# Moving low-part subtractions and a few sums from GpSimd to VectorE in a hybrid decoder layer

## The chip, the core and the metric

The program runs on one core of one Trainium2 chip. Its metric is the device time of one execution in microseconds (us); the time of the kernel is the median over several executions. A core has five engines with a queue of instructions each: TensorE (PE in the profile; its weight loads, which overlap the products, stand as PEld), VectorE (DVE), ScalarE (ACT), GpSimd (POOL) and SyncE (SP, which here only issues transfers). An engine works its queue in order; an instruction that waits holds up all that stand behind it.

## The reference

One layer for 1024 new prompt tokens and 8 x 4 decode tokens, width 1024:

```python
h = rmsnorm(x, rms1_g) * (1 + sc1) + sh1          # sc, sh, g: adaLN, silu(c) @ w_ada + b_ada
z = h @ w_in + b_in                               # q, k, v, f, GLU a and b, gate_a, gate_b
o = attend(q, k, v, log_sigmoid(z_f))             # 8 heads of 64, forgetting attention
y_a = o @ w_pa
u = glu_a * sigmoid(glu_b)
y_b = silu(layernorm(depthwise_causal_conv(u, 31 taps))) @ w_pb + b_pb
m = sigmoid(gate_a) * y_a + sigmoid(gate_b) * y_b
x = x + g1 * (m @ w_o)
h2 = rmsnorm(x, rms2_g) * (1 + sc2) + sh2
x = x + g2 * ((silu(h2 @ w_gate) * (h2 @ w_up)) @ w_ffn_out)
y = rmsnorm(x, final_g)                           # k, v, log f and the last rows of u go out too
```

The decode tokens attend to 1024 cached rows each, fetched by a page table.

## The kernel before

All data stand transposed: 128 features on the partitions, tokens along the free dimension (1056 columns, in blocks of 384, 384 and 288). To reach fp32 accuracy at a fast rate, each matrix product is made of three fp32r products: a weight tile w is split into a high part wh (rounded by ScalarE, line 315) and a low part wl = w - wh (line 318), the activations likewise into ah and al, and mm3 (lines 327 to 329) adds wh*ah, wh*al and wl*ah. So each weight tile passes through a transfer into wr (three buffers), a cast on ScalarE, a subtraction on VectorE or GpSimd, and then TensorE, whose third product is the first that needs wl. wh and wl have two buffers each, so a tile's low part may be written as soon as TensorE is done with the tile before the last.

The engine of the subtraction is the argument `eng` of split_w, which w_in_tile, gate, glu and branch hand down. A second argument names the queue that issues the transfer of the raw weights (GpSimd's or SyncE's).

The stages in program order: norm and modulation of x; q and k; v and the forget gates; glu(0); the decode attention in two groups (decode_group); glu(1) to glu(3) with gate(15) to gate(10) between; the prompt attention (scores and weighted, 32 units) with conv_ln, the layer norm of the convolution, at three of its units; gate(9) to gate(0) without 7, and four adaLN products among them; branch(1), the convolution's projection with its gate (out_b); gate(7); branch(0), the attention's projection with its gate and the sum of the two branches (out_a); the product with w_o; the FFN. glu also runs the depthwise convolution on VectorE: 30 multiply-adds over 1024 columns per channel tile (line 528, tile acc), marked as of low urgency, to run where VectorE has nothing else. conv_ln needs all four channel tiles.

The instructions don't stand in program order in the queues. The framework plans them: it simulates the program with estimated durations, and gives each engine's instructions in the order of that simulation; split_ahead marks the splits as urgent, so they stand ahead of what the program has before them. Which order results for another assignment of engines can't be read from the code.

out_a works per tile of 128 features and 264 columns on zg, the sigmoid of the gate, which lies in one of four buffers (tag gev): product times zg on VectorE (line 967), plus X(j), the other branch, on GpSimd for the first seven of eight tiles (line 968), high part on ScalarE (969), low part on VectorE (970).

Of the kernel before, what the change touches and what calls it, by code (L numbers as in the profile page):

```python
# [13 lines left out]
OP = mybir.AluOpType  # L14
# [15 lines left out]
KD = D // P  # L30
# [56 lines left out]
def hybrid_step(ctx, tc, xT, cT, vec, bvf, con, stT, ptab, ptabr, kcT, vc, lfc, w_ada, w_in, w_vfa, w_vfb,  # L87
# [132 lines left out]
            pe.matmul(prs[-1][:, to:to + m], ones[:m, :], dg[:m, d:d + m], start=True, stop=True)  # L220
        return prs if n > 512 else prs[0]

    def sumsq(tiles, n, eng=dve):
        s = sm.tile([P, 400], F32, name="ssum", tag="ssum", bufs=2)
        for i, t in enumerate(tiles):
            if i == 0:
                act.activation(s[:, :n], t, AF.Square)
            else:
                q = ev(sm, "sq", 2, (P, 400))
                act.activation(q[:, :n], t, AF.Square)  # L230
                eng.tensor_tensor(s[:, :n], s[:, :n], q[:, :n], OP.add)
        return s


# [260 lines left out]
    def glu(ct):  # L495
        u = cvp.tile([P, UW], F32, name="u", tag="u", bufs=2)
        us = u[:, KL + NP:].rearrange("p (b i) -> p b i", b=DB)
        pool.memset(u[:, 0:KL], 0.0)
        sp.dma_start(us[:, :, 0:KL], stT[ct].rearrange("p (b i) -> p b i", b=DB))
        wb = w_in_tile(12 + ct, pool, pool)  # L500
        sg = []
        for c in range(3):
            n = CH[c][1]
            ps = gemm_a(wb, c)
            t = ev(cvp, "sg", 4)
            act.activation(t[:, :n], ps[:, :n], AF.Sigmoid, bias=V[:, V_BB + ct:V_BB + ct + 1])
            sg.append(t)
        wa = w_in_tile(8 + ct, pool, pool)
        for c in range(3):
            o, n = CH[c]  # L510
            npr = min(n, NP - o)
            ps = gemm_a(wa, c)
            ba = V[:, V_BA + ct:V_BA + ct + 1]
            dve.scalar_tensor_tensor(u[:, KL + o:KL + o + npr], ps[:, :npr], ba, sg[c][:, :npr],
                                     op0=OP.add, op1=OP.mult)
            if n > npr:
                dve.scalar_tensor_tensor(us[:, :, KL:], ps[:, npr:n].rearrange("p (b t) -> p b t", t=DT), ba,
                                         sg[c][:, npr:n].rearrange("p (b t) -> p b t", t=DT),
                                         op0=OP.add, op1=OP.mult)
        act.dma_start(ucp[ct], u[:, NP:NP + KL])  # L520
        act.dma_start(ucs[ct].rearrange("p (b i) -> p b i", b=DB), us[:, :, DT:])
        with tc.high_priority(offset=-3000):
            a = cvp.tile([P, T], F32, name="acc", tag="acc", bufs=2)
            b = V[:, V_DWB + ct:V_DWB + ct + 1]
            wv = V[:, V_DW + ct * KC:V_DW + (ct + 1) * KC]
            dve.tensor_scalar(a[:, :NP], u[:, 0:NP], wv[:, 0:1], b, OP.mult, OP.add)
            for j in range(1, KC):
                dve.scalar_tensor_tensor(a[:, :NP], u[:, j:j + NP], wv[:, j:j + 1], a[:, :NP],  # L528
                                         op0=OP.mult, op1=OP.add)

            pr = cvp.tile([P, DB, KC], F32, name="cpr", tag="cpr", bufs=2)
            as_ = a[:, NP:].rearrange("p (b t) -> p b t", t=DT)
            for t in range(DT):
                dve.tensor_tensor(pr, us[:, :, t:t + KC], wv.unsqueeze(1).broadcast_to([P, DB, KC]), OP.mult)
                dve.tensor_reduce(as_[:, :, t], pr, mybir.AxisListType.X, OP.add)
            dve.tensor_scalar(a[:, NP:], a[:, NP:], b, None, OP.add)
        act.dma_start(acD[ct], a)
# [213 lines left out]
        decode_group(g)  # L751

    glu(1)
    gate(15, pool, pool)
    glu(2)
    gate(14, pool, pool)
    gate(13, pool, pool)
    glu(3)
    for i in (12, 11, 10):
        gate(i, pool, pool)  # L760

    cvp.release()
    dcp.release()
# [3 lines left out]
    def conv_ln(c):  # L767
# [4 lines left out]
            sp.dma_start(t, acD[ct][:, o:o + n])  # L772
            xc.append(t)
        s = sm.tile([P, 400], F32, name="lnsum", tag="ssum", bufs=2)
        pool.tensor_tensor(s[:, :n], xc[0], xc[1], OP.add)
        for ct in (2, 3):
            pool.tensor_tensor(s[:, :n], s[:, :n], xc[ct], OP.add)
        dve.tensor_scalar(s[:, :n], s[:, :n], 1.0 / CW, None, OP.mult)
        pm = ps_st()
        pe.matmul(pm[:, :n], ones, s[:, :n], start=True, stop=True)  # L780
        for ct in range(4):
            dve.tensor_tensor(xc[ct], xc[ct], pm[:, :n], OP.subtract)
        pr = rstd(sumsq(xc, n, pool), n, CW)
        for ct in range(4):
            g = V[:, V_LNG + ct:V_LNG + ct + 1]
            b = V[:, V_LNB + ct:V_LNB + ct + 1]
# [126 lines left out]
    for x in ready:  # L913
        weighted(*x)
    for i in (9, 8, 6, 5, 4, 3, 2, 1, 0):
        gate(i, pool, sp)
        if 3 <= i < 7:
            ada(8 - i, wp, "wr", 3, ps_mm)
    gains(1, V_RMS2, 32)
# [29 lines left out]
    def branch(which, src, w_p, width, out):  # L949
        xs = split_act(src)  # L950
        for j in range(KD):
            w = split_ahead(w_p[j], 4, pool)
            for o in range(0, T, width):
                zg = ev(wp, "gev", 4)[:, :width]
                sp.dma_start(zg, gD[which][j][:, o:o + width])
# [9 lines left out]
    def out_a(j, o, ps, zg):  # L965
        h, l = [merged(o // SUP, r, j)[:, o % SUP:o % SUP + HS] for r in range(2)]
        dve.tensor_tensor(zg, ps, zg, OP.mult)
        (pool if j < KD - 1 else dve).tensor_tensor(zg, zg, X(j)[:, o:o + HS], OP.add)
        act.copy(h, zg)
        dve.tensor_tensor(l, zg, h.bitcast(F32), OP.subtract)  # L970

    branch(1, cvD, w_pb, CW3, out_b)

    gate(7, pool, sp)
    ap.release()

    bp = mkpool(name="bp", bufs=1, side="right")
# [431 lines left out]
```

## Time and profile before

| | |
|---|---|
| time, median of 3 runs | 1636.25 us (1630.43 to 1641.71) |
| the profiled execution: its time, its span | 1629.88 us, 1628.1 us |
| TensorE busy with products | 1564.1 us, 96% of the span |
| VectorE, ScalarE, GpSimd busy | 1048.5, 697.3, 178.2 us |
| granted TensorE clock, mean | 0.992 of full speed |

The span runs from the first to the last instruction; the 1.8 us around it belong to the start and the end of the execution. Busy TensorE time counts products that overlap in its pipeline, so 96% isn't a share of peak. For each wait the profile names what ended it. The chain of work that ended last is followed back from the last instruction, at each step to what released it. Times in views are counted from the span's start.

### The profile page before, as it was taken

Reading aid. Unit: us, or ns where it says so; the run is one execution under the profiler, and the core shown is the slowest. Engines: PE = TensorE matmul, PEld = TensorE weight load, DVE = VectorE, ACT = ScalarE, POOL = GpSimd, SP = SyncE. Lnnn points to the kernel's source line nnn. Section 1 sums busy time; section 2 is a strip of 40 time slices with the busy share of each in tenths; the row PEclk is TensorE's granted clock in tenths of the full one; section 3 lists DMA queues with packets and bytes.
Section 4 is the critical chain, followed back from the end, with each engine's and each line's share of the span. In section 5 each row is a group of like instructions: output and inputs, shape, how many; then the busy total and the mean of one; then the engine's idle time right before and its main releaser. Section 6 shows DMA issues by size and latency. Waiting matters only on the chain.

```text
span 1628.1 us, 29682 instructions
## 1 busy us (share of the span) xinstructions
PE 1564.1 (96%) x11280; PEld 1475.9 (91%) x11280; DVE 1048.5 (64%) x2161; ACT 697.3 (43%) x1398; POOL 178.2 (11%) x147
## 2 busy tenths in 40 slices
PE   6999999999999989999999999999999999999997
PEld 4899978788977878999899989999999999999997
DVE  6942469999888867244559995555555596324644
ACT  4552112121376766434426663333333375224342
POOL 2121022342220101024200000000000000000000
PEclk9999999999999999999999999999999999999998
DMA  9195476777787774453554322222222257424552
GB/s 358 65 305 177 144 218 184 249 243 201 213 235 242 210 211 153 143 175 114 185 175 150 120 88 92 80 79 80 79 79 80 79 184 242 129 82 142 187 178 81
DMA packets 141424, 261.86 MB, mean 161 GB/s; under 512 B 24634, under 2 KB 81594, under 8 KB 140642
## 3 DMA queue, kind: packets, MB, share of 16 engines
q1 hardware_dynamic: 102802, 209.37, 41.0%
q10 hardware_dynamic: 36384, 43.01, 7.6%
q0 software_dynamic: 2096, 7.60, 1.5%
q8 instruction: 88, 1.44, 0.4%
q14 instruction: 54, 0.44, 0.1%
HBM read 206.44 MB, written 53.48 MB: 160 GB/s over the span
## 4 chain that ended last, share of the span: by engine, by line
PE 72%; DVE 12%; DMA 7%; ACT 3%; issue 3%; POOL 2%; SPq 1%; ACTq 0%; DVEq 0%; POOLq 0%
PE mm L1177 25%; PE mm L1278 16%; PE mm L329 7%; PE mm L328 7%; PE mm L327 7%; DVE acc L528 4%; DMA wa<-w_ada 2%; DMA gev<-gD 2%; POOL wl L318 1%; PE ptr L874 1%; PE mm L561 1%; PE mm L560 1%; PE mm L562 1%; DMA sq<-hD 1%; PE ppv L887 1%
## 5 line engine op out<-in xcount | busy, mean ns | idle before, releaser
L327 PE MATMUL mm<-ah,wh 128*128 128x384 f32 (+2 forms) x768 | 252.9, 330 | 8.8 <-ACT gev L384 4.0
L1278 PE MATMUL mm<-f,wo 128*128 128x352 f32 x1584 | 256.8, 323 | 0.0
L1278 PEld LDWEIGHTS mm<-f,wo 128*128 128x128 f32 x1584 | 254.8, 188 | 0.0
L329 PE MATMUL mm<-ah,wl 128*128 128x384 f32 (+2 forms) x768 | 251.5, 329 | 2.2 <-POOL wl L318 2.2
L328 PE MATMUL mm<-al,wh 128*128 128x384 f32 (+2 forms) x768 | 252.6, 329 | 0.0
L1177 PE MATMUL mm<-c,wc 128*128 128x264 f32 x1776 | 235.3, 285 | 1.5 <-ACT gev L1182 0.9
L1177 PE MATMUL mm<-b,wc 128*128 128x264 f32 x1680 | 228.1, 286 | 3.7 <-DVE wc L1135 1.5
L1177 PEld LDWEIGHTS mm<-c,wc 128*128 128x128 f32 x1776 | 224.1, 188 | 2.4 <-ACT gev L1182 1.3
L1177 PEld LDWEIGHTS mm<-b,wc 128*128 128x128 f32 x1680 | 214.7, 189 | 5.1 <-ACT wc L1134 2.0
L528 DVE SCALAR_TENSOR_TENSOR acc<-u,vec,acc 128x1024 f32<-128x1024 f32 x120 | 173.9, 1471 | 1.2
L327 PEld LDWEIGHTS mm<-ah,wh 128*128 128x128 f32 x768 | 145.9, 190 | 18.3 <-issue 5.9
L328 PEld LDWEIGHTS mm<-al,wh 128*128 128x128 f32 x768 | 146.3, 190 | 11.2 <-issue 10.4
L318 POOL TENSOR_TENSOR wl<-wr,wh 128x1024 fp32r<-128x1024 f32 (+1 forms) x44 | 111.8, 2545 | 396.0 <-ACT wh L315 340.9
L1229 DVE TENSOR_TENSOR wo<-wr,wo 128x512 fp32r<-128x512 f32 x108 | 69.7, 646 | 129.5 <-ACT wo L1228 128.9
L329 PEld LDWEIGHTS mm<-ah,wl 128*128 128x128 f32 x768 | 146.1, 190 | 6.3 <-POOL wl L318 3.1
L1134 ACT CAST wc<-wr 128x512 fp32r<-128x512 f32 x144 | 88.6, 621 | 141.4 <-PE mm L1177 132.4
L1228 ACT CAST wo<-wr 128x512 fp32r<-128x512 f32 x108 | 63.2, 585 | 150.6 <-PE mm L1278 143.3
L1135 DVE TENSOR_TENSOR wc<-wr,wc 128x512 fp32r<-128x512 f32 x144 | 98.5, 689 | 36.0 <-ACT wc L1134 35.0
L315 ACT CAST wh<-wr 128x1024 fp32r<-128x1024 f32 (+1 forms) x64 | 59.7, 939 | 93.1 <-PE mm L328 56.6
L192 POOL MEMSET rv<- 128x5 f32 x7 | 0.7, 103 | 746.2 <-DVE rt L210 746.2
L329 PE MATMUL mm<-b,wl 128*128 128x264 f32 x256 | 72.3, 286 | 2.2 <-DVE wl L318 2.2
L327 PE MATMUL mm<-b,wh 128*128 128x264 f32 x256 | 72.9, 285 | 1.3 <-ACT wh L315 1.3
(294 smaller groups left out, 2735.5 us busy)
## 6 DMA issues: line engine op xcount, KB each, us to landing
wr<-w_fi SPq DMA_DIRECT2D x52, 512.0 KB
wa<-w_ada SPq DMA_DIRECT2D x48, 512.0 KB
wr<-w_fo SPq DMA_DIRECT2D x36, 512.0 KB
kt<-kcT SPq DMA_DIRECT2D x64, 256.0 KB
vt<-vc SPq DMA_DIRECT2D x64, 256.0 KB
hD<-h ACTq DMA_DIRECT2D x44, 264.0 KB
wr<-w_in SPq DMA_DIRECT2D x18, 512.0 KB
wr<-w_o SPq DMA_DIRECT2D x16, 512.0 KB
```

Source lines behind the costliest of these rows:

```text
L315: d = act.copy(wh[:, r, :], raw[:, r, :])
L318: eng.tensor_tensor(wl[:, r, :], raw[:, r, :], wh[:, r, :].bitcast(F32), OP.subtract)
L327: pe.matmul(ps[:, :n], wh[:, k, :], xh, start=(k == 0), stop=False)
L328: pe.matmul(ps[:, :n], wh[:, k, :], xl, start=False, stop=False)
L329: pe.matmul(ps[:, :n], wl[:, k, :], xh, start=False, stop=(k == nk - 1))
L528: dve.scalar_tensor_tensor(a[:, :NP], u[:, j:j + NP], wv[:, j:j + 1], a[:, :NP], op0=OP.mult, op1=OP.add)
L1134: act.copy(w[:, 0, :n], raw)
L1135: dve.tensor_tensor(w[:, 1, :n], raw, w[:, 0, :n].bitcast(F32), OP.subtract)
L1177: pe.matmul(ps[:, :HS], w[i][:, r, k * P:(k + 1) * P], x[s][:, k, :], start=(new and k == 0 and j == 0), stop=(k == 3 and j == 2), skip_gr ...
L1228: act.copy(x[:, 0, :], raw)
L1229: dve.tensor_tensor(x[:, 1, :], raw, x[:, 0, :].bitcast(F32), OP.subtract)
L1278: pe.matmul(ps[e][:, :n], w[r][:, k * P:(k + 1) * P], f[x], start=(k0 + k + i == 0), stop=(k0 + k == HT - 1 and i == 2))
```

## The change

Five places hand `dve` where `pool` stood. The transfers that GpSimd's queue issues stay on GpSimd's queue; the first four tiles of q and k (first_w), the second halves of split_shifted and the copies of q and k stay on GpSimd too.

```diff
-    def sumsq(tiles, n, eng=dve):
+    def sumsq(tiles, n):
...
-                eng.tensor_tensor(s[:, :n], s[:, :n], q[:, :n], OP.add)
+                dve.tensor_tensor(s[:, :n], s[:, :n], q[:, :n], OP.add)
...
-        wb = w_in_tile(12 + ct, pool, pool)
+        wb = w_in_tile(12 + ct, dve, pool)
...
-        wa = w_in_tile(8 + ct, pool, pool)
+        wa = w_in_tile(8 + ct, dve, pool)
...
-    gate(15, pool, pool)
+    gate(15, dve, pool)
...
-    gate(14, pool, pool)
-    gate(13, pool, pool)
+    gate(14, dve, pool)
+    gate(13, dve, pool)
...
-        gate(i, pool, pool)
+        gate(i, dve, pool)
...
-        pool.tensor_tensor(s[:, :n], xc[0], xc[1], OP.add)
+        dve.tensor_tensor(s[:, :n], xc[0], xc[1], OP.add)
         for ct in (2, 3):
-            pool.tensor_tensor(s[:, :n], s[:, :n], xc[ct], OP.add)
+            dve.tensor_tensor(s[:, :n], s[:, :n], xc[ct], OP.add)
...
-        pr = rstd(sumsq(xc, n, pool), n, CW)
+        pr = rstd(sumsq(xc, n), n, CW)
...
-        gate(i, pool, sp)
+        gate(i, dve, sp)
...
-            w = split_ahead(w_p[j], 4, pool)
+            w = split_ahead(w_p[j], 4)
...
-        (pool if j < KD - 1 else dve).tensor_tensor(zg, zg, X(j)[:, o:o + HS], OP.add)
+        dve.tensor_tensor(zg, zg, X(j)[:, o:o + HS], OP.add)
...
-    gate(7, pool, sp)
+    gate(7, dve, sp)
```

## Rows read from the trace of the kernel before

**Rows 1.** Busy time by stage; columns: stretch, length, busy us of each engine (instructions)
```profile
244.00:428.00 184.00, 178.97 (x1157) 151.94 (x1154) 181.56 (x193) 36.51 (x58) 55.09 (x22) 0.99 0.75 228
428.00:465.00 37.00, 35.40 (x243) 32.59 (x243) 28.82 (x95) 22.00 (x43) 6.22 (x6) 1.00 0.52 152
465.00:660.00 195.00, 184.16 (x1345) 155.90 (x1339) 147.16 (x472) 131.06 (x270) 25.55 (x21) 0.98 0.70 208
660.00:742.00 82.00, 79.85 (x504) 78.31 (x503) 27.34 (x38) 34.01 (x58) 15.01 (x11) 1.00 0.51 164
742.00:800.00 58.00, 54.02 (x431) 52.52 (x430) 32.55 (x67) 29.52 (x73) 30.89 (x35) 1.00 0.45 136
```

**Rows 2.** What TensorE waited for from 206 to 428 us: total, times, longest
```profile
PE pss L692 <- DMA kt<-kcT: 3.1, 2, 1.9
PE mm L329 <- POOL wl L318: 2.2, 1, 2.2
```

**Rows 3.** What TensorE waited for from 428 to 660 us
```profile
PE mm L161 <- DMA wa<-w_ada: 5.6, 5, 2.5
PE ptr L874 <- DVE ptl L877: 2.7, 3, 2.1
PE pst L780 <- DVE lnsum L778: 1.6, 1, 1.6
```

**Rows 4.** What TensorE waited for from 660 to 800 us
```profile
PE mm L329 <- POOL wl L318: 2.8, 4, 1.2
PE mm L329 <- DVE wl L318: 1.7, 2, 0.9
```

**Rows 5.** The page's span, and its group of the convolution's multiply-adds
```profile
span 1628.1 us, 29682 instructions
...
L528 DVE SCALAR_TENSOR_TENSOR acc<-u,vec,acc 128x1024 f32<-128x1024 f32 x120 | 173.9, 1471 | 1.2
```

**Rows 6.** The chain that ended last, its pieces from 424 to 438 us
```profile
424.72 3.31 DVE acc L528
428.05 3.08 DMA acD<-acc
...
437.34 0.91 PE pst L780 x2
```

**Rows 7.** GpSimd in order of time: start, us, line, operation, idle before
```profile
322.14 16.62 POOL L318 TENSOR_TENSOR wl<-wr,wh 128x1024 fp32r<-128x1024 f32 x1 [16.69 <-ACT wh L315]
...
385.77 3.10 POOL L318 TENSOR_TENSOR wl<-wr,wh 128x1024 fp32r<-128x1024 f32 x1 [16.61 <-ACT wh L315]
```

**Rows 8.** VectorE in order of time, the same stretches
```profile
320.93 15.63 DVE L528 SCALAR_TENSOR_TENSOR acc<-u,vec,acc 128x1024 f32<-128x1024 f32 x13
...
386.54 3.41 DVE L528 SCALAR_TENSOR_TENSOR acc<-u,vec,acc 128x1024 f32<-128x1024 f32 x1
...
390.19 1.27 DVE L528 SCALAR_TENSOR_TENSOR acc<-u,vec,acc 128x1024 f32<-128x1024 f32 x1
```

**Rows 9.** Tile acc, its multiply-adds; columns: shortest/median/longest ns, first and last start
```profile
L528 DVE SCALAR_TENSOR_TENSOR acc<-u,vec,acc x120: 1248/1278/3410, 224.0 to 424.7; 128x1024 f32<-128x1024 f32 x120
```

**Rows 10.** Line 318 on VectorE: durations, and VectorE's idle time before it
```profile
L318 DVE TENSOR_TENSOR wl<-wr,wh x20: 1208/1224/1399, 79.2 to 881.5; 128x1024 fp32r<-128x1024 f32 x20
...
  ACT wh L315: 6.6, 10
```

**Rows 11.** Groups of GpSimd by shape: count, busy, mean ns, idle before
```profile
L318 POOL TENSOR_TENSOR wl<-wr,wh 128x1024 fp32r<-128x1024 f32 x28 | 90.3, 3229 | 326.5 <-ACT wh L315 287.9 <-PE pss L818 15.1 <-DMA vt<-vc 13.2
L318 POOL TENSOR_TENSOR wl<-wr,wh 128x512 fp32r<-128x512 f32 x16 | 21.5, 1347 | 69.6 <-ACT wh L315 52.9 <-PE mm L329 16.6
L968 POOL TENSOR_TENSOR gev<-gev,XA 128x264 f32<-128x264 f32 x16 | 12.9, 813 | 10.5 <-DVE gev L967 6.1 <-ACT b L969 2.8 <-ACT wh L315 1.5
L231 POOL TENSOR_TENSOR ssum<-ssum,sq 128x384 f32<-128x384 f32 x6 | 6.3, 1044 | 5.5 <-ACT sq L230 5.2
```

**Rows 12.** Groups of VectorE by shape, for the prices there
```profile
L1135 DVE TENSOR_TENSOR wc<-wr,wc 128x512 fp32r<-128x512 f32 x144 | 98.5, 689 | 36.0 <-ACT wc L1134 35.0
L394 DVE TENSOR_TENSOR qkl<-gev,qkh 128x384 fp32r<-128x384 f32 x8 | 4.4, 555 | 14.4 <-ACT qkh L393 14.3
L968 DVE TENSOR_TENSOR gev<-gev,XB 128x264 f32<-128x264 f32 x4 | 1.6, 426 | 0.0
```

**Rows 13.** Line 825 on VectorE, a one-column instruction of the attention: shortest/median/longest ns
```profile
L825 DVE SCALAR_TENSOR_TENSOR st<-mx,Cq x64: 190/212/2348, 429.6 to 646.7; 128x1 f32<-128x1 f32 x64
```

**Rows 14.** The chain that ended last, shares of its stretch from 680 to 800 us
```profile
by line: DMA gev<-gD 21.3%; issue 16.1%; PE mm L329 11.6%; PE mm L328 11.4%; PE mm L327 10.4%; ACT b L969 3.4%; DMA gD<-gev 3.3%; ACT gev L956 3.1%; DMA yr<-cvD 3.0%; POOL gev L968 2.7%; POOL wl L318 2.5%; DVE gev L967 2.5%; ACT wh L315 2.5
```

## What the change does to the time, predicted before it ran

> **What bounds the kernel now.** I read the busy time by stage first. In the stages that hold the moved work, from 244 to 800 us, TensorE has an instruction running nearly all the time [rows 1]: 178.97 of 184 us, 35.40 of 37, 184.16 of 195, 79.85 of 82, 54.02 of 58. So the change can win at most TensorE's idle time there, 5.0 + 1.6 + 10.8 + 2.2 + 4.0 = 23.6 us, and only the part that GpSimd or VectorE causes. The second thing to see is VectorE, with 181.56 of 184 us busy in the first of these stages: it is the full engine there, beside a full TensorE, while GpSimd is busy for 55.09 us and idle for most.
>
> Then the waits of TensorE say which of its idle time has to do with the change. From 206 to 428 us it waited 2.2 us for a low part from GpSimd and 3.1 us for pages of the cache [rows 2]; from 428 to 660 us 5.6 us for adaLN weights, 2.7 us for low parts of the attention's probabilities, 1.6 us for the layer norm's sum [rows 3]; from 660 to 800 us 2.8 us for low parts from GpSimd and 1.7 us for those of w_o [rows 4]. The transfers aren't touched. What is named with GpSimd or hangs on it is 2.2 + 1.6 + 2.8 = 6.6 us.
>
> Last the two engines beside each other. A multiply-add of the convolution takes 1278 ns in the median, but 1471 on average, and the longest 3410 [rows 5, 9]. The row at 386.54 shows why: 3.41 us, while GpSimd has its subtraction from 385.77 on; the one at 390.19, with GpSimd idle, takes 1.27 us [rows 7, 8]. The other way round, GpSimd's subtraction at 322.14 takes 16.62 us, while VectorE runs 13 multiply-adds one behind the other from 320.93 to 336.56 [rows 7, 8]. So each of the two holds the other up: both read two tiles in SBUF, and they take turns by whole instructions.
>
> **The change part by part.** Moved are 24 full low parts (8 of GLU, 16 of the gates), 16 half ones (branches), 18 sums of the layer norm and 28 of the first branch: 86 instructions. No transfer moves; GpSimd's transfers now wait for VectorE's low part instead of its own, with three buffers ahead, and I cost that at nothing.
>
> Low parts beside the convolution. 15 of the 24 run between 206 and 428 us. On GpSimd a full one takes 3229 ns on average [rows 11], on VectorE 1224 ns in the median [rows 10]. Added to VectorE: 15 x 1.22 = 18.3 us. Given back: what the multiply-adds were held up, 120 x (1471 - 1278) ns = 23.2 us [rows 5, 9]. Net 4.9 us less. Bounds: 18.3 us more, if nothing is given back, and 23.2 us less, if the new instructions were free. I take the net, since the 3.41 us row stands beside GpSimd's and the 1.27 us row doesn't. On the end it is worth little, as TensorE is full in this stage: I take 1 us, from nothing to 4.9. The wait of 2.2 us goes in full: the part that took 16.62 us would take 1.2, in its place in VectorE's queue.
>
> Layer norm. The chain that ended last runs from the last multiply-add at 424.72 over two transfers and the sums to TensorE's mean at 437.34 [rows 6]. Of the first mean's wait 1.6 us stands with the sum. The three additions ahead of it take about 1.0 us each on GpSimd, as line 231 does (1044 ns), and 0.56 on VectorE (a 128x384 subtraction, 555 ns) [rows 11, 12]: 3 x 0.49 = 1.5 us earlier, if VectorE's queue lets them in at once. I take 1.6 us gone, from 0 to 1.6.
>
> In the attention (428 to 660 us) VectorE gets up to 18 x 0.56 + 6 x 1.22 = 17.4 us more. What it gets back is uncertain. Line 825, an instruction on one column, has a median of 212 ns and a longest of 2348 [rows 13], so it too is held up by GpSimd at times; six low parts by 2.1 us each (2348 - 212) would be 12.8 us, the lower bound is nothing. I take half: 11 us more, most of it in the stage from 465 to 660 us, where VectorE goes from 147 to some 156 of 195 us. TensorE waits for VectorE there by the rows, so some of it shows; bounds 0 and 11 us; I take +2, as 2.7 us is all that it waits for the probabilities' low parts now.
>
> Branches (660 to 800 us). A half low part goes from 1347 to 689 ns, and no longer stands in one queue with the sums; a sum goes from 813 to 426 ns [rows 11, 12]. The wait of 2.8 us loses 2.0 (between 0 and 2.8). The sums stand in a ring of four buffers: a gate's tile is loaded, used, and its buffer freed when line 970 is done. The load of gev is the largest part of the chain here, 21.3% [rows 14], so the ring sets the pace beside TensorE. One turn serves four tiles; 28 sums are seven turns, each shorter by 0.39 us: 2.7 us, at most the 4.0 us that TensorE idles from 742 to 800 us, from which the 1.7 us for w_o's low parts come too [rows 1, 4]. I take 2 (0 to 2.7). Is VectorE full then? 32.55 + 28 x 0.43 + 7 x 0.69 = 49 of 58 us: not quite.
>
> Waits in VectorE's order. On GpSimd a low part that stood waiting for its cast held up nothing else: 287.9 us of idle time ahead of 28 of them [rows 11]. On VectorE the multiply-adds and the attention stand behind it, and TensorE waits for those. VectorE's own low parts cost 6.6 us of idle time over 20 [rows 10], 0.33 us each. The 21 between 206 and 660 us make 6.9 us at that; TensorE is full for most of it. I take +1, from 0 to 6.9.
>
> The sum: -2.2 - 1 - 1.6 + 2 - 2.0 - 2 + 1 = -5.8 us. The profiled execution took 1629.88 us, 1.8 more than its span [rows 5]; it becomes 1624. It lies 6.4 us under the median of the runs shown, 1636.25, and about at their fastest; I put the same distance to the median of the new kernel: 1636.25 - 5.8, some 1630 us.
>
> **The rivals.**
>
> Carried through. The relief of VectorE lets the prompt attention start earlier, and the planned order, which now has all of this work on one engine, fits the run better. For it: VectorE has 181.56 of 184 us busy, and the chain runs over its multiply-adds. The most is TensorE's idle time of 23.6 us less the transfers, 5.6 + 3.1: 14.9 us [rows 1 to 3]. Against it: TensorE is full in 428 to 465 us too. About 1621 us.
>
> Nothing comes through. TensorE's waits go, and others of the same 6 us take their place, as the queues are planned anew; for it speaks that TensorE is full everywhere, against it that the waits of [rows 2, 4] have one cause, GpSimd, that is gone: 1635 us.
>
> VectorE is full, and GpSimd's help is gone. The Trainium skill, "Perfetto Trace Analysis", section "Optimizing Scalar/DVE Operations", says that where VectorE is saturated, giving some of its work to GpSimd may make sense, though the two share a read port and it might not help; this change does the reverse. In rows: 18.3 us are added to a stage in which VectorE has 2.4 us free, and if nothing is given back, the layer norm and the attention come 16 us later. TensorE has 35 us of work in 428 to 465 us to run meanwhile, so I count half: +8, less the 6 of the other terms' gains, plus what the attention lacks then, 7: about 1645 us. The row of 3.41 us speaks against it.
>
> Slower: VectorE stands waiting for casts. The place is VectorE's queue from 206 to 660 us, with 21 low parts planned by estimated times. With w us of waiting each, the convolution ends 15w - 4.9 later and the attention loses 6w. Up to w = 0.3 that is hidden; at w = 1.5 it is 17.6 + 9 less 6: 20 us slower, 1656 us. From about 1.3 on it is over 1%. For it: GpSimd idled some 10 us per low part for the casts; against it: the 0.33 us of VectorE's own.
>
> **How the numbers follow.** Forecast 0.48, carried through 0.22, nothing 0.14, VectorE full 0.06, waiting for casts 0.10. One per cent, 16 us, is about what a measurement of this kernel can tell from no change, as its runs lie from 1630.43 to 1641.71 us. Faster by more: 0.20, most of the second case. Slower by more: 0.12, the last case and a little of the fourth. Within 1%: 0.68. The range goes from 1612 us, under the second case by half the spread of the runs shown and a little more, to 1645 us, the fourth; left out are the last case and the tails, some 0.18.
>
> **What the profile would show.** If the steps hold: no multiply-add of line 528 over 1.5 us, its mean within 30 ns of its median; line 318 on VectorE at 1.2 us; GpSimd busy for under 5 us from 244 to 428 us; the last multiply-add some 5 us earlier, against the stages ahead of it; no wait of TensorE for a low part over 1 us between 206 and 800 us; the stage with gev's ring some 2 us shorter. If VectorE waits for casts, its idle time ahead of line 318 is above 20 us in total. The prediction is wrong if multiply-adds stay long with GpSimd idle, if the attention's stage grows by more than 5 us, or if the planned order moves a stage as a whole, which nothing here can show beforehand.

## The result, and the profile after

The changed kernel took 1639.91 us (median of 20 executions, 1633.84 to 1646.41), the kernel before 1630.57 us beside it (20 executions, 1626.06 to 1641.71): a ratio of 1.0051, with a 95% interval of 1.0038 to 1.0063. By this ratio it is slower by 8.3 us (the two medians lie 9.3 us apart). The forecast was 5.8 us faster: the time lies within its range, the sign is wrong.

First the busy time of the changed kernel by stage, in the columns of [rows 1] (the last stage of before lies 8 us earlier):

```profile
244.00:432.00 188.00, 184.46 (x1206) 158.67 (x1207) 169.52 (x204) 38.25 (x61) 3.45 (x8) 1.00 0.75 224
432.00:469.00 37.00, 35.16 (x255) 28.90 (x255) 27.50 (x93) 19.02 (x39) 0.10 (x1) 1.00 0.71 209
469.00:669.00 200.00, 186.34 (x1339) 163.60 (x1337) 148.99 (x485) 128.15 (x263) 0.21 (x2) 0.97 0.67 191
669.00:700.00 31.00, 21.05 (x110) 19.15 (x109) 13.09 (x25) 18.64 (x33) 0.00 (x0) 0.78 0.37 109
700.00:750.00 50.00, 50.00 (x307) 49.67 (x306) 24.29 (x37) 19.91 (x34) 0.00 (x0) 1.00 0.54 167
750.00:808.00 58.00, 58.00 (x478) 58.00 (x477) 45.08 (x109) 32.16 (x77) 0.00 (x0) 1.00 0.52 158
```

Two branches are called the first in the texts on record: branch(0), where the 28 sums are meant, and branch(1), which runs before it, where the input is meant that line 944 splits. Here they go by their numbers.

Two stages stand out. The last, with branch(0)'s sums, has TensorE busy for 58.00 of 58 us, where it was 54.02 [rows 1]: that is the gain that was forecast. The fourth, 31 us around the end of the attention, has it busy for 21.05, at a granted clock of 0.78. The kernel before has nothing like it. Its own attention ends at 672 us (here 687), and of the 31 us around that, in the same columns, TensorE has 30.05, at full clock:

```profile
662.00:693.00 31.00, 30.05 (x192) 28.79 (x191) 9.69 (x13) 14.52 (x23) 2.94 (x3) 1.00 0.54 175
```

What the prediction said of the durations of single instructions came out. The span, the convolution's multiply-adds (page and tile acc, as [rows 5, 9]), line 825 (as [rows 13]) and, for later, the idle time of VectorE ahead of low parts (as [rows 10]), in the changed kernel:

```profile
span 1632.3 us, 29602 instructions
L528 DVE SCALAR_TENSOR_TENSOR acc<-u,vec,acc 128x1024 f32<-128x1024 f32 x120 | 150.0, 1282 | 0.7
L528 DVE SCALAR_TENSOR_TENSOR acc<-u,vec,acc x120: 1247/1282/1294, 218.2 to 431.3; 128x1024 f32<-128x1024 f32 x120
L825 DVE SCALAR_TENSOR_TENSOR st<-mx,Cq x64: 189/210/221, 434.0 to 670.3; 128x1 f32<-128x1 f32 x64
  ACT wh L315: 34.4, 24
```

With GpSimd nearly idle no multiply-add is longer than 1294 ns (it was 3410), and the one-column instruction of line 825 no longer than 221 ns (it was 2348). So GpSimd did hold VectorE up, and now it doesn't. And yet the last multiply-add ended at 432.6 us instead of 428.0.

To see where TensorE's time went I worked out its loss by stretch: for each product the distance to the start of the next, less what the same form of product usually takes in the trace of before (a third of its distances there are shorter), summed. It holds the waits and the half-speed stretches alike. "Around its end" runs from 15 us before the last weighted sum of the attention to 15 us behind the first product of branch(1). Each is one profiled execution:

| us lost by TensorE | up to decode | decode, convolution | attention | around its end | branches | rest | sum |
|---|---|---|---|---|---|---|---|
| before | 34.2 | 47.1 | 49.6 | 3.7 | 6.7 | 26.4 | 167.7 |
| after | 30.5 | 46.7 | 53.6 | 15.6 | 0.9 | 25.7 | 173.0 |

The sums differ by 5.3 us, the ends of the last products by 4.2. Ahead of decode the 3.7 us are no more than the scatter of single executions: e4 below, whose edit leaves that stretch alone, lies as far from the kernel before there. Of the rest, +11.9 us lie around the end of the attention, +4.0 in the attention, -5.8 in the branches. The +4.0 isn't clear of the scatter either: e4, e17 and e18 below have TensorE's order of before up to the branches, and lose 48.6 to 53.7 us in the attention. The profiled execution of the changed kernel, 1634.07 us, is a quick one: it shows about half of the 8.3 us. The other half goes with the mean granted clock, 0.982 over its 20 executions and 0.985 in the profiled one, against 0.988 for the kernel before over all executions beside these studies.

What happens at that end: TensorE of the changed kernel in order of time, all its pieces there that have a wait ahead of them (start, length, line, idle time and what ended it), and its stretch cut finer:

```profile
670.50 0.52 PE L874 MATMUL ptr<-con,px 128*128 128x128 f32 x3 [1.22 <-DVE st L825]
676.76 0.58 PE L886 MATMUL ppv<-pth,vh 128*128 128x256 f32 x1 [3.78 <-ACT pth L876]
679.77 1.11 PE L874 MATMUL ptr<-con,px 128*128 128x128 f32 x4 [0.85 <-DVE ptl L877]
684.49 0.39 PE L887 MATMUL ppv<-ptl,vh 128*128 128x256 f32 x1 [0.19 <-DVE ptl L877]
686.98 0.39 PE L886 MATMUL ppv<-pth,vh 128*128 128x256 f32 x1 [1.13 <-DVE ot L898]
690.41 2.13 PE L327 MATMUL mm<-yh,wh 128*128 128x352 f32 x6 [2.74 <-ACT yh L944]
```

```profile
669.00:676.00 7.00, 2.77 (x22) 2.28 (x20) 2.67 (x9) 6.89 (x14) 0.00 (x0) 0.99 0.32 94
676.00:683.00 7.00, 5.38 (x24) 4.68 (x25) 3.10 (x7) 5.17 (x11) 0.00 (x0) 0.52 0.04 9
683.00:690.00 7.00, 3.32 (x23) 2.59 (x21) 2.94 (x6) 3.00 (x6) 0.00 (x0) 0.96 0.47 140
690.00:697.00 7.00, 6.59 (x24) 6.59 (x25) 3.02 (x3) 2.50 (x3) 0.00 (x0) 0.55 0.54 167
```

The last units' chain (scores, maximum, exponential, transpose, weighted sum) and then the split of branch(1)'s input (line 944) have nothing of TensorE's to run beside them. In the 7 us from 669 TensorE is busy for 2.77, and in the next 7 the granted clock is 0.52, that is mostly the lower level, 1.2 GHz; it happens again from 683 to 697. So each gap is paid twice. The Trainium skill ("TensorE: Matmul & The Clock Gate", section "HAM oscillation — how this bites in real kernels") says of a long wait that the work behind it starts at the lower clock; this trace agrees, with 0.52 and 0.55.

Why nothing is there can be counted in TensorE's order of instructions. The gates' products (2232 ahead of gate 7's, which come later in both kernels) are what fills the attention. In the kernel before, 160 of them stand behind the attention's last score product and 45 behind its last weighted sum. In the changed kernel there are none behind either. The plan places each product at its estimated earliest time, and in the changed kernel they were all used up earlier.

### The profile page after: what moved, and what is told of

It is laid out like the page before. It is cut to its first block, busy times and chain, and to the rows that moved or that the text cites. A ratio compares the mean times of both kernels' runs of the same rounds, so it can differ in the third digit from the quotient of the medians.

```text
span 1632.3 us, 29602 instructions
## 1 busy us (share of the span) xinstructions
PE 1563.7 (96%) x11280; PEld 1478.4 (91%) x11280; DVE 1056.9 (65%) x2247; ACT 699.3 (43%) x1398; POOL 38.3 (2%) x61
## 4 chain that ended last, share of the span: by engine, by line
PE 81%; DMA 6%; DVE 5%; SPq 3%; issue 2%; ACT 2%; POOL 0%; ACTq 0%; DVEq 0%
PE mm L1177 26%; PE mm L1278 16%; PE mm L327 9%; PE mm L329 9%; PE mm L328 9%; DMA wa<-w_ada 3%; PE ptr L874 1%; SPq L631 1%; SPq L632 1%; PE mm L561 1%; PE mm L560 1%; PE mm L562 1%; PE ppv L887 1%; PE pss L815 1%; PE mm L161 1%
## 5 line engine op out<-in xcount | busy, mean ns | idle before, releaser
L528 DVE SCALAR_TENSOR_TENSOR acc<-u,vec,acc 128x1024 f32<-128x1024 f32 x120 | 150.0, 1282 | 0.7
L318 DVE TENSOR_TENSOR wl<-wr,wh 128x1024 fp32r<-128x1024 f32 (+1 forms) x60 | 64.5, 1080 | 34.7 <-ACT wh L315 34.4
L327 PE MATMUL mm<-b,wh 128*128 128x264 f32 x256 | 72.7, 285 | 0.5 <-ACT wh L315 0.5
L328 PE MATMUL mm<-b,wh 128*128 128x264 f32 x256 | 72.4, 283 | 0.0
```

The lines of the kernel that those rows point to most:

```text
L318: eng.tensor_tensor(wl[:, r, :], raw[:, r, :], wh[:, r, :].bitcast(F32), OP.subtract)
L327: pe.matmul(ps[:, :n], wh[:, k, :], xh, start=(k == 0), stop=False)
L328: pe.matmul(ps[:, :n], wh[:, k, :], xl, start=False, stop=False)
```

## The experiments

Each kernel ran in five rounds beside the kernel before; us against it are the ratio times the median of before in those runs. "Left" counts the gates' products in TensorE's order behind the last score product and, of these, behind the last weighted sum. "End" and "attention" are TensorE's losses as above, in the one profiled execution.

| kernel | moved to VectorE | left | us against before (95%) | attention, end: us lost |
|---|---|---|---|---|
| before | nothing | 160, 45 | | 49.6, 3.7 |
| after | all | 0, 0 | +8.3 (6.2 to 10.3) | 53.6, 15.6 |
| e1_glu_gates | GLU, six early gates | 12, 0 | +6.7 (3.9 to 9.5) | 49.7, 11.7 |
| e2_layer_norm | 18 sums of the layer norm | 164, 51 | +7.0 (4.4 to 9.8) | 66.7, 2.8 |
| e3_late_gates | ten late gates | 58, 0 | -0.3 (-2.6 to 2.0) | 48.3, 10.5 |
| e4_branches | branches | 160, 45 | -5.0 (-7.3 to -2.6) | 49.8, 3.1 |
| e5_means | 9 sums of the means | 107, 0 | +7.2 (4.2 to 10.1) | 53.5, 11.7 |
| e6_squares | 9 sums of squares | 192, 58 | -3.1 (-6.5 to 0.2) | 53.6, 2.1 |
| e7_loads_ahead | 18 sums, loads 3 units ahead | 167, 52 | +12.1 (7.7 to 16.5) | 68.0, 2.4 |
| e8_gates_held | all, gates 1 and 0 behind unit 26 | 119, 0 | +8.6 (5.5 to 11.7) | 62.7, 10.9 |
| e9_gates_last | all, gate 1 behind unit 28, 0 behind 31 | 144, 72 | 0.0 (-2.8 to 2.8) | 64.4, 1.6 |
| e10_means_gates_last | e5 held as e9 | 144, 72 | +2.6 (0.5 to 4.9) | 58.6, 3.3 |
| e11_all_but_means | all but the means | 19, 0 | -2.3 (-4.6 to 0.2) | 50.9, 11.8 |
| e12_branches_squares | e4 and e6 | 192, 58 | -7.7 (-10.4 to -4.9) | 54.1, 2.3 |
| e13_glu_gates_last | e1 held as e9 | 144, 72 | +2.4 (-0.5 to 5.5) | 60.3, 2.2 |
| e14_all_but_means_last | e11 held as e9 | 144, 72 | -2.4 (-4.9 to 0.0) | 60.5, 2.7 |
| e15_sums_gates_last | e2 held as e9 | 164, 72 | +12.7 (9.1 to 16.3) | 64.9, 0.8 |
| e16_first_mean_back | e9, first mean on GpSimd | 144, 72 | -1.0 (-3.6 to 1.6) | 58.8, 3.3 |
| e17_branch_low_parts | branches' low parts only | 160, 45 | -2.9 (-5.1 to -0.7) | 48.6, 2.1 |
| e18_branch_sums | branch(0)'s sums only | 160, 45 | -6.0 (-8.2 to -3.9) | 53.7, 3.8 |

**The change in four parts.** The theory at this point was that VectorE, which works its queue in order, stands waiting for casts and transfers and so loses its relief (theory 3 in the texts below). The rivals were the planned order (theory 1) and VectorE's load in the attention (theory 2). Each kernel is the one before with one part of the diff; of e1 and e4, for instance:

```diff
-        wb = w_in_tile(12 + ct, pool, pool)
+        wb = w_in_tile(12 + ct, dve, pool)
...
-    gate(15, pool, pool)
+    gate(15, dve, pool)
```
```diff
-            w = split_ahead(w_p[j], 4, pool)
+            w = split_ahead(w_p[j], 4)
...
-        (pool if j < KD - 1 else dve).tensor_tensor(zg, zg, X(j)[:, o:o + HS], OP.add)
+        dve.tensor_tensor(zg, zg, X(j)[:, o:o + HS], OP.add)
```

> Only the 14 low parts of GLU's and the six early gates' weights are on VectorE. Theory 1, the planned order: with more on VectorE beside the convolution the plan puts the attention later against the gates' products; in this kernel's planned order 12 gate products are left behind the last score product, in the kernel before 160, in the changed one none. Then the attention's end stands without other work for TensorE, as in the changed kernel, and this part alone costs 8 to 16 us (the changed kernel's attention ended 15.5 us later). Theory 2, VectorE is too full in the attention: this part puts nothing into the attention's stage, so -3 to +2 us. Theory 3, VectorE waits for casts: some 6 us of idle VectorE ahead of line 318, +3 to +6 us.

> Only the layer norm's 18 sums are on VectorE. Theory 1: the planned order keeps 164 gate products behind the last score product, as the kernel before (160), so -2 to +2 us. Theory 2: VectorE gets 10 us more in the attention, +3 to +6 us. Theory 3: nothing waits for casts here, 0.

> Only the low parts of gates 9 to 0 are on VectorE. Theory 1: 58 gate products are left behind the last score product where the kernel before has 160, none behind the last weighted product where it has 45: +2 to +6 us. Theory 2: 10 low parts, 12 us more on VectorE in and behind the attention, +3 to +6 us. Theory 3: +2 to +4 us with VectorE's idle time ahead of line 318 over 5 us.

> Only the branches' half low parts and the 28 sums of the first branch are on VectorE. All theories: TensorE's planned order up to the branches is that of the kernel before; the stage from the first out_b to the last out_a took 110.7 us in the kernel before and 102.8 us in the changed one, so -4 to -8 us.

Two parts lose, one gains, one is nothing. That the late gates alone cost nothing (e3) was forecast by no theory, and e3 loses 10.5 us of TensorE's time at the end of the attention all the same. The parts' sum, 6.7 + 7.0 - 0.3 - 5.0 = +8.4, agrees with the whole by chance, as e11 will show.

**Means, squares, loads ahead.** e5 moves lines 775 and 777 alone, e6 line 783 alone. In e7 the transfers of xc are issued three units before the sums:

```diff
+            conv_load(n // 8)
+        if n in (3, 11, 19):
             conv_ln(n // 8)
```

> Of the change only the nine additions ahead of the layer norm's means (lines 775 and 777) go to VectorE; the nine additions of squares stay on GpSimd. If VectorE stands waiting for the transfers of xc (the layer norm's inputs) with the softmax behind it, these nine carry the loss of the eighteen: +5 to +7 us against the kernel before, with several us of idle time of VectorE at line 775 from 428 to 660 us. If it is only VectorE's load, they are half of it: +3 to +4 us, and no idle time at line 775. If it is the place that the plan gives the second and third layer norm, the time follows where their mean products lie: as before (437, 480, 531 us) no loss, later ones a loss.

> Of the change only the nine additions of squares of the layer norm go to VectorE; the nine ahead of the means, which are what waits for the transfers, stay on GpSimd. If waiting for the transfers of xc carries the loss: 0 to +1 us. If VectorE's load does: +3 to +4 us. If the place of the layer norms in the plan does, the time follows that place, +7 us if the second and third come 13 to 18 us later as they did with all eighteen sums.

> All eighteen sums of the layer norm on VectorE, as in the run of the layer norm alone, which was 7.0 us slower; but the transfers of xc are issued three units of the attention ahead of the sums (units 0, 8, 16; the sums at 3, 11, 19), so that VectorE needn't wait for them. If the wait for the transfers is the cause: no idle time of VectorE at lines 775 to 783 over 1 us, and a time within 2 us of the kernel before. If VectorE's load is: still +6 to +7 us. The gates' products that the plan leaves behind the last scores (167 of 2232) are as before (160), so the tail of the attention is no matter here.

The means carry the loss, the squares none: VectorE's load alone is out, as both are nine additions of one size. But e7 didn't take the wait away as meant: VectorE still stood 3.6 us for the first xc (the last multiply-add ends only at 426.7 us), and the kernel came out no faster than e2. It speaks for no theory.

**Gates held back.** In e8 and e9 nothing is moved between engines; the last gates' products are given a later place on TensorE. e8 has `done_v[26]` for both, e9:

```diff
         times_v(*held[0])
+        done_v.append(nc.cur_bb.bb.instructions[-1])
...
-        gate(i, dve, sp)
+        with tc.issue_after(done_v[(31, 28)[i]]) if i < 2 else nullcontext():
+            gate(i, dve, sp)
```

> The changed kernel, with one thing more: the products of the last two gates (1 and 0) are held back on TensorE until the weighted unit number 26 of the attention is done, so that 119 of them lie behind the last scores, where the changed kernel has none and the kernel before has 160. If the missing products of the gates in the tail of the attention are a part of the loss, TensorE's idle time from 669 to 690 us shrinks from some 11 us to under 4 and 4 to 7 us of the 8.3 come back. If the loss is VectorE's waits and load alone, the time stays within 1.5 us of the changed kernel, as the products are only run later.

> The changed kernel, with the products of gate 1 held back on TensorE behind the weighted sums of unit 28 of the attention and those of gate 0 behind those of unit 31, the last: the plan then leaves 72 of the gates' 2232 products behind the last scores and 72 more behind the last weighted sum, where the run before this one left 119 and none, the changed kernel none and none, and the kernel before 115 and 45. If what counts is that TensorE has work left while the first branch's input is split behind the attention (line 944), TensorE is busy for 25 to 27 of 28 us around the end of the attention, where it was for 19, its clock doesn't fall there, and 5 to 8 us come back: 1632 to 1635 us. If the loss is VectorE's waits and load, the time stays at 1638 to 1641 us.

e9 takes the whole 8.3 us back, e8 nothing, which is what was expected of e8 if VectorE's waits and load were the loss. Both have products left behind the last score (119 and 144); only e9 has some behind the last weighted sum. TensorE around that end in e8 and e9 (31 us each, columns as above), and its one wait there in e8:

```profile
684.00:715.00 31.00, 23.18 (x135) 22.90 (x134) 11.11 (x15) 13.06 (x19) 0.00 (x0) 0.83 0.50 156
```
```profile
699.68 2.13 PE L327 MATMUL mm<-yh,wh 128*128 128x352 f32 x6 [7.82 <-ACT yh L947]
```
```profile
669.00:700.00 31.00, 30.80 (x201) 30.54 (x199) 10.48 (x14) 13.78 (x22) 0.00 (x0) 1.00 0.54 171
```

In e8 the gap became one wait of 7.82 us for branch(1)'s input, whose buffers the code allocates after it has given up the attention's; in e9 gate 0 runs in it, and the clock stays at full level. Of TensorE's loss there the table says the same without an exception: the six kernels with no product left behind the last weighted sum lose 10.5 to 15.6 us at that end, the others 0.8 to 3.8. Of the time it doesn't: e3 and e11 lose 10.5 and 11.8 us there and are no slower than the kernel before. And e9 loses 14.0 us less at the end than the changed kernel, but 10.8 us more in the attention. The two traces together show 3.5 us of the 8.3 (1634.07 against 1630.53 us); the rest lies in executions that weren't profiled.

**The parts again with the hold.** e10 and e13 to e15 are the kernels of the same parts with e9's lines; e11 is the changed kernel with lines 775 and 777 as before, e16 is e9 with those on GpSimd for the first layer norm only (`me = pool if c == 0 else dve`).

> The nine additions ahead of the means on VectorE, as in the run that was 7.6 us slower, and gates 1 and 0 held back as in e9_gates_last (72 and 72 products). In the run without that, TensorE waited 6.9 us for the first branch's input (line 944) at half clock behind it. If the products left for that place are the cause, the loss goes: -1 to +2 us against the kernel before. If VectorE waiting for the transfers of xc is, it stays at +6 to +8 us.

> The changed kernel with the nine additions ahead of the layer norm's means back on GpSimd. The plan leaves 19 products of the gates behind the last scores and none behind the last weighted sum, about as in the changed kernel. If the parts add up by what each does to its own engine: 8.3 - 7.6, some +1 us, 1631 to 1633 us. If the place of the gates' products carries the loss: still +5 to +8 us, 1636 to 1639 us.

> GLU's and the six early gates' low parts on VectorE, as in the run that was 6.7 us slower, with gates 1 and 0 held back as in e9_gates_last (72 products behind the last scores and 72 behind the last weighted sum, where that run had 12 and none). If that run lost at the end of the attention alone, the prediction's terms for this part (-2.2 for the wait, -1 of relief, +1 for waits for casts: -2.2 in sum) show: -4 to 0 us against the kernel before. If VectorE's waiting for casts in its own order (17 us of idle time in the stage with the convolution) is what costs, it stays at +4 to +7 us.

> The changed kernel with the nine additions ahead of the means back on GpSimd and gates 1 and 0 held back as in e9_gates_last. Without holding it was 2.3 us faster than the kernel before, though TensorE lost 11.8 us around the end of the attention, where e9_gates_last lost 1.6. If that loss can be taken back here as well: -8 to -11 us, 1620 to 1623 us, and the means on VectorE cost 8 to 11 us in the middle of the attention. If it is hidden here: -1 to -4 us.

> Only the eighteen sums of the layer norm on VectorE, which was 7.0 us slower though its plan leaves 113 products behind the last scores and 51 behind the last weighted sum, with gates 1 and 0 held back (92 and 72). The end of the attention is filled in both, so the loss should stay at +5 to +8 us if it lies in the middle of the attention (the clock, and TensorE waiting for VectorE's maxima and scaled probabilities); a fall to under +2 us would say that it was the end after all.

> As e9_gates_last, with the three additions ahead of the first layer norm's mean alone back on GpSimd (3 of 9); VectorE stood 3.5 us waiting for a transfer there with the first units' softmax behind it. If that wait is what the means cost: as e14, 1620 to 1624 us. If it is the six later additions, or the place that the plan gives the layer norms: as e9, 1630 to 1632 us.

The means lose 4.6 of their 7.2 us by the hold, GLU and early gates 4.3 of 6.7 (here the two intervals overlap): about this much of both lay at the attention's end. What is left is 2.6 and 2.4; for GLU and the early gates neither expectation met that. For the means another pair gives as much, 2.4 us between e9 and e14, both held, but their intervals overlap. Of the first mean alone (e16) -1.0 can't be told from either.

Two kernels limit the theory. e11 has no product left behind the last weighted sum and loses 11.8 us at the end, and is still 2.3 us faster by its median, where +1 or +5 to +8 was expected; holding the gates (e14) takes 9.1 us of loss away there and adds 9.6 in the attention, where the held products are now missing: no gain. A loss at the end is thus partly a loss moved there. So the changed kernel's loss hangs on two things at once, the missing products and the means on VectorE: taking back either one alone removes it (e9, e11), and both together (e14) give no more than e11. How the means make the gap cost time isn't shown. And the eighteen sums alone (e2, e15) lose without any gap at the end: +17.1 and +15.3 us in the attention against before, and e15's +12.7 us are more than the +5 to +8 that were expected. TensorE there, 430 to 660 us, in the kernel before and in e15, and what it waited for in e2 from 428 to 686 us:

```profile
430.00:660.00 230.00, 217.56 (x1571) 186.49 (x1570) 174.41 (x560) 152.41 (x311) 31.78 (x27) 0.99 0.67 198
```
```profile
430.00:660.00 230.00, 209.31 (x1474) 176.37 (x1473) 179.82 (x572) 145.89 (x299) 12.32 (x8) 0.95 0.66 191
```
```profile
PE mm L161 <- DMA wa<-w_ada: 9.8, 7, 2.3
PE ptr L874 <- DVE px L831: 3.1, 1, 3.1
PE ppv L886 <- DVE ot L898: 2.7, 2, 1.6
PE pss L815 <- DVE mx L820: 2.2, 2, 1.5
...
```

In e15 TensorE starts 97 products fewer in the stretch and is busy 8 us less, at a clock of 0.95 instead of 0.99; in e2 there are more waits for adaLN weights (9.8 us, 5.6 before, [rows 3]) and some for VectorE's softmax. In e2 the second and third means also come at 493 and 550 us, 13 and 18 later than before. That they come late isn't the cause by itself: in e11, e14 and e16 they come at 496 to 504 and 546 to 555 us, without a loss. What of the rest is cause and what effect stays open.

**Branches.** The best of all is the two gaining parts together, and e17 and e18 halve the branches' part.

> Only the branches' low parts, the first branch's sums and the layer norm's sums of squares on VectorE: the two parts that gained by themselves, 5.0 and 2.1 us. The plan leaves 134 products of the gates behind the last scores and 58 more behind the last weighted sum, so no loss is expected there by either theory. If the gains add: -5 to -7 us, 1624 to 1626 us; if they hide one another: -3 to -5 us.

> Of the branches' part only the sixteen half low parts go to VectorE; the 28 sums stay on GpSimd. By the prediction's terms: TensorE's wait of 2.8 us for GpSimd's low parts goes, -2.0 us (0 to -2.8). If the low parts stood behind the sums in GpSimd's queue and the whole gain of 5.0 us comes from there: -4 to -5 us.

> Of the branches' part only the 28 sums go to VectorE; the low parts stay on GpSimd, whose queue then holds nothing else there. By the prediction's terms: -2 us (0 to -2.7) from the ring of four buffers, and TensorE's wait for GpSimd's low parts stays at 2 to 3 us. If it was the sums that held up the low parts in GpSimd's queue: -4 to -5 us, and that wait is gone too.

What TensorE waited for from 676 to 810 us in e17 and e18, the first lines of each (in e4 no wait of one kind is above 0.6 us):

```profile
PE mm L329 <- DVE wl L318: 1.1, 2, 0.7
PE mm L327 <- ACT wh L315: 0.8, 2, 0.6
```
```profile
PE mm L329 <- POOL wl L318: 2.7, 3, 1.2
PE mm L327 <- ACT yh L944: 1.2, 1, 1.2
```

e18 keeps the wait of 2.7 us for GpSimd's low parts and is the faster half all the same. It isn't a shorter turn of gev's ring that makes it so. The products of line 327 in branch(0), with their first and last start, in the kernel before, e18, e17 and e4:

```profile
L327 PE MATMUL mm<-yh,wh x128: 278/285/291, 740.9 to 789.6; 128*128 128x264 f32 x128
L327 PE MATMUL mm<-yh,wh x128: 278/285/390, 740.8 to 789.8; 128*128 128x264 f32 x128
L327 PE MATMUL mm<-yh,wh x128: 278/285/291, 736.2 to 782.5; 128*128 128x264 f32 x128
L327 PE MATMUL mm<-yh,wh x128: 278/285/291, 737.6 to 783.9; 128*128 128x264 f32 x128
```

They take 49.0 us with the sums moved alone, 48.7 before and 46.3 in the two kernels with the low parts moved: the stretch of the ring is shortened by the low parts. What the sums gain lies behind it, in the first tiles of the product with w_o. What TensorE waited for there, from the end of branch(0) on for 50 us, in the kernel before (789 to 840 us) and in e17 (782 to 832 us); e18 (789 to 840) and e4 (783 to 833) have no wait there at all:

```profile
PE mm L329 <- DVE wl L318: 1.7, 2, 0.9
PE mm L327 <- ACT wh L315: 0.7, 2, 0.6
```
```profile
PE mm L329 <- DVE wl L318: 1.1, 2, 0.7
PE mm L327 <- ACT wh L315: 0.6, 1, 0.6
```

By TensorE's loss as above, the low parts gain 2.4 us among branch(0)'s products (2.6 before, 0.2 in e17, 2.9 in e18) and the sums 3.5 us in the 20 us behind them (3.5 before, 2.6 in e17, none in e18); e4 has 0.2 and none. So in the traces the halves add. Whether the times do can't be told: -2.9 and -6.0 stand against -5.0, each with some 2 us of uncertainty. Why w_o's low parts come in time once the sums leave GpSimd wasn't tried. e12, at 1624.3 us, beats both the kernel before and the changed one; of its gates' products 58 stay behind the last weighted sum.

## Why the prediction was wrong, step by step

**The step that failed** is that the sum has no term for the end of the attention. Its terms go over the waits that the trace of before shows, and there TensorE doesn't wait, since the gates' products fill it: 30.05 us of 31. They are a reserve that the plan had left there, 45 products behind the last weighted sum, and it was gone in the changed kernel: 3.7 us of loss became 15.6. e9, which changes only the place of gates 1 and 0, gives the 8.3 us back. That is not the whole miss: e9 stands at 0.0, and the forecast at -5.8; what is left lies, by its trace, in the attention (64.4 us lost against 49.6). Nor has the gap a price of its own, since e11 has it too and, with the means back on GpSimd, is not slower than the kernel before; what the sum lacks is a term for the gap and the means together. The prediction had named "if the planned order moves a stage as a whole" as what would make it wrong, without a price. A bound was to be had: if those 31 us lose all of their filler, TensorE stands for the length of the chain of the last units and of the branch's input.

**Relief of VectorE, -1.** The stretches were given back as forecast, 23.9 us by the page's row (173.9 to 150.0). But the convolution didn't end earlier: from decode's first product to the last multiply-add it took 219.1 us instead of 209.8. What VectorE waited for in the changed kernel from 213 to 433 us:

```profile
DVE u L514 <- PE mm L329: 7.2, 3, 3.2
DVE wl L318 <- ACT wh L315: 5.8, 5, 2.7
DVE dt L700 <- PE pss L692: 4.9, 3, 3.2
DVE cpr L534 <- DMA u<-stT: 3.6, 1, 3.6
DVE cr L705 <- ACT dt L704: 1.6, 1, 1.6
...
```

In the kernel before, from 218 to 428 us, those were 2.6 for u and 1.0 for dt, and nothing else. A VectorE that lags finds everything ready; one that keeps up stands at what comes next in its order. TensorE's loss in this stretch was 47.1 and is 46.7 us: the relief was worth nothing, and the wait of 2.2 us for GpSimd's low part went without a gain, as others took its place.

**Waits for casts, +1 (0 to 6.9).** From 206 to 660 us they are 5.8 + 0.7 = 6.5 us: the estimate of 6.9 us was right, and TensorE didn't lose by it in the convolution. The bound that the prediction set, 20 us of idle time ahead of line 318, was badly set: the 34.4 us counted include 15.9 from before 206 us and 12.0 behind 660. The rival that stands waiting for casts didn't come about.

**Layer norm, -1.6.** Wrong in sign. The first mean's product came 9.3 us behind the last multiply-add and now comes 11.5 behind it (444.1 against 432.6). VectorE itself stood for the transfer at the first sum, with the softmax behind it:

```profile
437.80 0.56 DVE L775 TENSOR_TENSOR lnsum<-xc 128x384 f32<-128x384 f32 x1 [3.54 <-DMA xc<-acD]
```

In the changed kernel the means cost 10.6 us (against e11); alone on VectorE 7.2 us (e5). With the gates held it is 2.4 us (e9 against e14), which isn't clear of the noise.

**Attention, +2, VectorE 11 us fuller.** The size of VectorE's part was off. From the last multiply-add to the last weighted sum it is busy for these us, in the kernel before, the changed one and e9 (columns as above):

```profile
428.00:672.00 244.00, 231.56 (x1669) 200.49 (x1667) 178.53 (x571) 157.53 (x321) 33.06 (x28) 0.99 0.65 194
```
```profile
432.60:687.40 254.80, 232.10 (x1653) 201.34 (x1651) 184.18 (x597) 161.14 (x326) 0.31 (x3) 0.96 0.64 184
```
```profile
431.60:676.70 245.10, 224.04 (x1582) 191.12 (x1580) 179.97 (x595) 152.25 (x315) 0.31 (x3) 0.95 0.64 183
```

That is 5.7 and 1.4 us more, where 11 were forecast; of the 17.4 us added, 11.7 to 16.0 came back. The stage is 10.8 us longer all the same, as TensorE is idle in it for 22.7 us instead of 12.4; a stage longer by more than 5 us was one of the prediction's signs of being wrong. In e9 it is as long as before, but with 21.1 us idle and 87 products fewer in it. The Trainium skill ("Perfetto Trace Analysis", section "Optimizing Scalar/DVE Operations") speaks of handing work of a saturated VectorE to GpSimd; the change takes it back. The rival with that mechanism, 1645 us, lies near the time that came out, but the mechanism isn't there: VectorE is busy for 169.52 of 188 us in the convolution, where it was for 181.56 of 184.

**Branches, -2.0 and -2.** Right in sum and direction: -4.0 forecast, -5.0 measured in e4, and 5.8 us less of TensorE's loss in the changed kernel. The low parts came out as reasoned, 2.9 us by time and 2.4 by TensorE's loss. The term for the ring was right by luck: with the sums moved alone the stretch of the ring stays as long as it was, and their gain is the wait for w_o's low parts behind it, of which the prediction had seen 1.7 us [rows 4] and left them out.

**The base.** The forecast of 1630 us was counted from 1636.25, the median of three runs; over twenty it is 1630.57. So the 1630 us lie at the time of before, and only the difference can be judged.

## What to carry to other kernels

Where a planner orders the instructions, count what stands behind the last product of each latency-bound stage before you change an engine's durations; that filler is as much a part of the stage as its waits, and a trace of before shows it only as busy time. What it is worth has to be measured: here putting it back gave 8.3 us in one kernel (e9) and nothing in another (e14 against e11). Relief of an in-order engine is worth something only where the bounding engine waits for it; elsewhere it turns into waiting at the next instruction. Test parts with the filler held in place, since the parts' own sum can agree with the whole by chance: here +8.4 and +8.3, while the whole without the means was -2.3, where the sum has +1.

## What the runs showed of the hardware

How much of the time is TensorE's clock was not expected. The share of the clock not granted, times the span, is (1 - 0.9824) x 1638 = 29 us for the changed kernel and (1 - 0.9885) x 1630 = 19 us for the one before: 10 us more, of the order of the 8.3 us lost, though not all of it is time in which TensorE had work. In e9, at 0.9864, it is 22 us.

In the gap of the changed kernel ScalarE changes three times between the sigmoid of the branch's gate (line 956) and the attention's exponential (line 826), with a table load of 1.28 us each. In order of time:

```profile
671.87 1.28 ACT L956 ACT_TABLE_LOAD   x1
673.16 0.50 ACT L956 ACTIVATE gev<-gev 128x352 f32<-128x352 f32 x1
...
674.45 1.28 ACT L826 ACT_TABLE_LOAD   x1
675.75 0.51 ACT L826 ACTIVATE py<-py,st 128x256 f32<-128x256 f32 x1
...
676.25 0.46 ACT L876 CAST pth<-ptr 128x384 fp32r<-128x384 f32 x1
676.73 1.28 ACT L956 ACT_TABLE_LOAD   x1
```

The first two stand in ScalarE's queue ahead of the copy of pth, at 676.25, for which TensorE waited 3.78 us. The kernel before changes once there, at 681.14 us, 9 us behind its last weighted sum. The Trainium skill ("ScalarE: Activation LUTs", section "What ACT_TABLE_LOAD costs") has 1283 ns for the load, as here, and some 1380 ns more for a drain at every change; here the load starts where the activation ahead of it ends (671.87 behind 671.85 us), and the next activation at the end of the load. What these loads alone cost wasn't tried; but e1, e3 and e11 load once in that stretch, and still lose 10.5 to 11.8 us at the end, against 15.6.
